# Seven half products for eight in five projections of the last two token groups

## The chip, the cores and the metric

The kernel runs on one core of a Trainium2 chip. The metric is device time in microseconds for one execution. A core has TensorE (matmuls, PE in the profile), VectorE (DVE), ScalarE (ACT), GpSimd (POOL) and SyncE (SP), which issues all DMAs of this kernel. Each engine works through its own instructions in order; they meet through semaphores.

## What is computed

One step of a decoder layer on 2,064 prompt positions (16 meta tokens among them) and 8 x 8 sampled ones, model width 1,024, all in fp32. Cut to what matters here:

```python
proj = rmsnorm(h, norm_gain) @ w_in             # 1024 -> 6 x 1024
u_s, z_s, u_p, z_p, gates = split(proj)         # gates = sigmoid(.. + b_gate) -> g_s, g_p
y_s = ssm_branch(u_s)                           # scan, gelu, y * sigmoid(y @ w_glu + b_glu)
y_p = pool_branch(u_p)                          # running means over 2, 4, 8, 16 rows, a 256 x 256 mix each
merged = g_s * ((y_s * silu(z_s)) @ w_branch_ssm) + g_p * ((y_p * silu(z_p)) @ w_branch_pool)
out = rmsnorm(h + merged @ w_out, final_norm_gain)
```

The projections for u_p, z_p, z_s, g_p and g_s are those that the change touches.

## The kernel before

**Tiling.** Features lie on the 128 partitions, tokens on the free axis. The tokens are four groups (g0 to g3, `GROUPS`) of 544, 536, 536 and 512 columns. An output block of 128 features of a projection is one *unit*: eight input blocks, three matmuls each (`mm3`), since every fp32 operand is split in a high and a low part and high x high, high x low and low x high are summed. A group of 536 columns is done as two outputs of 268, so a unit is 48 matmuls; the group of 512 takes 24. Results go to a PSUM tile `acc` of [128, 2, 512] f32, of which there are three (`acc`, `proj`).

**Weights.** The weights of each unit come from HBM as one raw tile of 512 KB (`w_load`, three buffers), ScalarE writes the high part (`w_high`, L105, tile wh), VectorE the low part (`w_low`, L207, tile wl), three buffers each. For unit i+2, `w_high` stands at the start of unit i and `w_low` at its end, and the load of unit i+5 at its end.

**Order.** All instructions are written in one hand-made order. `units` lists the matmul units. For each the main loop writes: `w_high` of the unit two ahead, the post work of the unit before (PSUM to SBUF, nonlinearity), events (`at`), and the unit's matmuls, between which `between` places small steps at given fractions (`at_part`).

**Stages of a group.** `u_pool`: units up (u), zp (z), the first gates (g) and the mixes (m) in the order of `ORDER`; a whole pooling of an up block on VectorE is written in one go in the post work (`up_post`), and the pooled block is split two units later (`po_split`). `u_pgate`: branch products brp with the remaining gates. `u_zs`: zs, with the GELU of the state-space output beside it (ScalarE, VectorE and GpSimd in a chain). `u_rest`: glu, gates gs with products brs, and eight out units, in which the inputs of the next group are normalised and split (`x_norm`); the norm of the outputs follows two units later. The final division goes with the next group's first units.

**State-space rounds.** The scan over groups 0 and 1 is round 0, that over groups 2 and 3 round 1. A round is 38 ticks of small matmuls and steps on all engines, spread over units by `spread`. Round 1 runs from the end of g0 to the `u_pgate` stage of g2, with weight 0 (BB) in the pool stages: 98 units that count.

## Time and profile before

| | us |
|---|---|
| runs (3) | 2111.9, 2112.03, 2113.97 |
| median | 2112.03 |
| profiled execution | 2110.94 |
| its span, first to last instruction | 2109.2 |

In that span TensorE was busy for 2068.6 us (98%), VectorE for 1311.9 (62%), ScalarE for 1007.5 (48%), GpSimd for 541.0 (26%); the mean granted TensorE clock was 0.995. A busy share says how much of the time an engine had an instruction in it. Matmuls overlap, so the length of one is longer than its spacing to the next; the spacing is what counts in a row of them. Groups 2 and 3 fill about the last 850 us: up to some 1680 us matmuls of 268 columns, from there of 512.

### The profile page before, as it was taken

How to read it: one execution, taken by the hardware profiler on the slowest of the kernel's cores; microseconds unless marked ns; L12 is line 12 of the kernel's file. 1: busy time of each engine (PE TensorE's matmuls, PEld its weight loads, DVE VectorE, ACT ScalarE, POOL GpSimd, SP SyncE). 2: the span in 40 equal slices, each digit the busy share in tenths (PEclk: the TensorE clock that was granted, in tenths of full speed). 3: DMA queues.
4: the chain of work that ended last, by engine and by line, in shares of the span. 5: the costliest groups of instructions: out<-in, count | busy, mean ns of one | idle time of the engine just before them, and what ended most of it. 6: DMA issues, size and time to landing. Idle time of an engine off the chain costs nothing.

```text
span 2109.2 us, 37669 instructions
## 1 busy us (share of the span) xinstructions
PE 2068.6 (98%) x14968; PEld 1960.0 (93%) x14968; DVE 1311.9 (62%) x1844; ACT 1007.5 (48%) x1579; POOL 541.0 (26%) x718
## 2 busy tenths in 40 slices
PE   7999999999999999999899999999999999999998
PEld 7998899998999999999899999999999988888887
DVE  6879858898655776546755776535533667345344
ACT  5334469877555553356665553324332333234322
POOL 1156525463422330023422330012100210022001
PEclk9999999999999999999999999999999999999999
DMA  5435557587534643245444533334233443343333
GB/s 202 145 124 171 172 163 212 158 244 203 156 92 143 177 135 121 91 124 141 119 128 147 166 117 127 96 116 125 91 106 124 134 133 105 108 144 105 100 99 101
DMA packets 226095, 288.30 MB, mean 137 GB/s; under 512 B 111744, under 2 KB 156160, under 8 KB 225920
## 3 DMA queue, kind: packets, MB, share of 16 engines
q1 hardware_dynamic: 225920, 285.90, 44.8%
q8 instruction: 118, 1.93, 0.4%
q14 instruction: 57, 0.47, 0.1%
HBM read 242.58 MB, written 40.89 MB: 134 GB/s over the span
## 4 chain that ended last, share of the span: by engine, by line
PE 85%; DVE 5%; ACT 4%; DMA 2%; issue 2%; POOL 1%; SPq 0%; DVEq 0%; ACTq 0%; POOLq 0%
PE acc L128 27%; PE acc L132 27%; PE acc L130 27%; PE ps_k L408 1%; PE sx L519 1%; PE sy L589 1%; PE sy L590 1%; ACT wh L105 1%; DVE sX L549 1%; DVE w L951 1%; DVE wl L207 0%; DMA ys<-sS 0%; DVE sph L506 0%; DMA smc<-mat_d 0%; DVE sX L537 0%
## 5 line engine op out<-in xcount | busy, mean ns | idle before, releaser
L128 PE MATMUL acc<-ah,wh 128*128 128x268 f32 (+4 forms) x4504 | 1055.2, 304 | 9.1 <-ACT wh L105 7.8
L132 PE MATMUL acc<-ah,wl 128*128 128x268 f32 (+4 forms) x4504 | 1045.7, 302 | 0.0
L130 PE MATMUL acc<-al,wh 128*128 128x268 f32 (+4 forms) x4504 | 1044.4, 301 | 0.0
L128 PEld LDWEIGHTS acc<-ah,wh 128*128 128x128 f32 x4504 | 726.2, 189 | 43.2 <-issue 8.0
L105 ACT ACTIVATE wh<-raw 128x1024 fp32r<-128x1024 f32 (+1 forms) x336 | 347.3, 1034 | 854.5 <-PE acc L130 559.8
L132 PEld LDWEIGHTS acc<-ah,wl 128*128 128x128 f32 x4504 | 725.1, 189 | 27.1
L130 PEld LDWEIGHTS acc<-al,wh 128*128 128x128 f32 x4504 | 725.4, 189 | 26.7 <-DVE al L720 0.2
L207 DVE TENSOR_TENSOR wl<-raw,wh 128x1024 fp32r<-128x1024 f32 (+1 forms) x336 | 421.6, 1256 | 139.4 <-ACT wh L105 138.2
L541 POOL TENSOR_TENSOR sXw<-sXw,sph 128x270 f32<-128x270 f32 (+1 forms) x64 | 46.5, 726 | 362.5 <-ACT sXw L527 362.3
L872 DVE SCALAR_TENSOR_TENSOR H<-H,acc 128x536 f32<-128x536 f32 (+2 forms) x64 | 44.9, 702 | 85.8 <-ACT H L871 85.7
L970 DVE SCALAR_TENSOR_TENSOR H<-po,H 128x536 f32<-128x536 f32 (+2 forms) x32 | 22.7, 711 | 111.2 <-ACT po L968 107.5
L946 POOL TENSOR_SCALAR w<-w 128x536 f32<-128x536 f32 (+2 forms) x32 | 27.0, 845 | 227.6 <-ACT w L945 227.4
L114 DVE TENSOR_TENSOR al<-H,ah 128x536 fp32r<-128x536 f32 (+3 forms) x96 | 77.4, 842 | 7.7 <-ACT ah L105 6.7
L537 DVE TENSOR_TENSOR sX<-sx,scc 128x270 f32<-128x270 f32 (+1 forms) x64 | 27.1, 423 | 85.9 <-ACT sxs L530 59.9
L549 DVE TENSOR_TENSOR_SCAN sX<-r,state,sX 128x135 f32<-128x135 f32 (+1 forms) x128 | 72.8, 609 | 2.3
L1011 POOL TENSOR_TENSOR ss<-ss,po 128x536 f32<-128x536 f32 (+2 forms) x25 | 41.8, 1673 | 125.6 <-ACT po L1007 107.0
L827 POOL COPY hist<-E 128x16 f32<-128x16 f32 x24 | 15.6, 651 | 218.8 <-ACT E L817 218.8
L836 DVE TENSOR_TENSOR w<-E 128x483 f32<-128x483 f32 (+2 forms) x32 | 22.6, 708 | 78.8 <-ACT E L817 54.4
L981 DVE SCALAR_TENSOR_TENSOR sg<-sg,acc 128x536 f32<-128x536 f32 (+2 forms) x32 | 22.4, 701 | 78.1 <-PE acc L132 78.1
L105 ACT ACTIVATE ah<-H 128x536 fp32r<-128x536 f32 (+3 forms) x80 | 50.2, 644 | 43.1 <-DVE H L902 31.9
L923 DVE SCALAR_TENSOR_TENSOR G<-sg,acc 128x536 f32<-128x536 f32 (+2 forms) x32 | 22.4, 701 | 74.9 <-PE acc L132 70.9
L103 POOL TENSOR_SCALAR ah<-G 128x536 fp32r<-128x536 f32 (+2 forms) x16 | 14.9, 943 | 193.2 <-DVE sg L981 150.8
(231 smaller groups left out, 2216.3 us busy)
## 6 DMA issues: line engine op xcount, KB each, us to landing
raw<-in_wb SPq DMA_DIRECT2D x318, 512.0 KB, 3.8
smc<-mat_d SPq DMA_DIRECT2D x64, 256.0 KB, 3.6
smb<-mat_d SPq DMA_DIRECT2D x64, 128.0 KB, 2.5
xr<-in_xb SPq DMA_DIRECT2D x21, 268.0 KB, 4.2
H<-in_xb SPq DMA_DIRECT2D x19, 268.0 KB, 4.4
ys<-sS SPq DMA_DIRECT2D x32, 135.0 KB, 4.4
us<-po SPq DMA_DIRECT2D x16, 268.0 KB, 4.6
su<-us SPq DMA_DIRECT2D x64, 67.0 KB, 2.6
```

Source lines behind the costliest of these rows:

```text
L105: A.activation(out, in_, AF.Copy)
L114: V.tensor_tensor(l, x, h.bitcast(F32), ALU.subtract)
L128: PE.matmul(out, wh, xh, start=first, stop=False)
L130: PE.matmul(out, wh, xl, start=False, stop=False)
L132: PE.matmul(out, wl, xh, start=False, stop=last)
L207: V.tensor_tensor(l[:, c], r[:, c], h[:, c].bitcast(F32), ALU.subtract)
L537: V.tensor_tensor(d["x"], d["px"][:, :, :g.kp], d["c"][:, :, 1:g.kp + 1], ALU.mult)
L541: G.tensor_tensor(d["xw"], d["xw"], d["s"][:, :, 1:g.kp + 1], ALU.mult)
L549: V.tensor_tensor_scan(x[:, j], r8[:, i].to_broadcast([P, g.kp]), x[:, j], state[:, i], ALU.mult, ALU.add)
L872: V.scalar_tensor_tensor(self.v3(out), self.v3(out), 1.0, self.pv(ps), ALU.add, ALU.mult)
L946: G.tensor_scalar(q, q, 0.044715, 1.0, ALU.mult, ALU.add)
L1011: (G if h is None else V).tensor_tensor(self.ss[:, c], self.ss[:, c], s, ALU.add)
```

## The change

For groups 2 and 3 the units of the five projections go in pairs of output blocks. A pair is a product of 2 x 2 blocks: two output blocks, two halves of the eight input blocks, two halves of the tokens (268 or 256 columns). Seven products of half size take the place of eight, on sums and differences of the operands.

- **Weights** (`ws_load`, `ws_sum`): for each pair VectorE makes four sums of weight blocks, in 40 jobs between the end of g0 and g1's first glu units, and stores them to DRAM (`ws_d`). A pair is four units of kind s (t = 0 to 3), the first three with a full tile of weights, the last with half; `w_load` gathers each from one to three DMAs.
- **Inputs** (`s_op`, `x_scale`): in the brs and out units of the group before, VectorE and ScalarE prepare seven input operands (b11, t1, t2, b22, t3, b21, t4) in place of one split.
- **Products** (`s_unit`): accumulators a and b are the two halves of one acc tile, c half of a second. a takes b11, t2, t3 and t4 in turn, and ScalarE copies it out after each of the first three (p1, u2, u3); c takes t1 (copied to p5) and b22; b takes b21. VectorE and ScalarE combine these in the post work.
- **Order** (`u_fast_pool`): pool stage by `FAST_ORDER`, with the zs pairs 0 and 1 moved into it; pooling is issued in single steps, 1.3 us apart by the plan's own lengths (`up_step`); zs pairs 2 and 3 follow the brp units. `w_low` of s units stands at 0.6 of the unit.
- **State-space round 1** now ends in g1 (77 units that count), its buffers are freed for the new tiles, and `final_states` runs in g1's first out unit.

**TensorE, g2, units zp 0 and up 1, before**: 48 matmuls a unit, then the next unit into another acc tile (ah, al: input parts, wh, wl: weight parts; the waits are for an engine's semaphore).

```order
L128 MATMUL acc_15154<-ah_14593,wh_15011 128x268 [waits DVE_49,Activation_49]
L128 MATMUL acc_15154<-ah_14593,wh_15011 128x268
L130 MATMUL acc_15154<-al_14594,wh_15011 128x268 x2
L132 MATMUL acc_15154<-ah_14593,wl_15066 128x268 x2
...
L128 MATMUL acc_15218<-ah_14593,wh_15070 128x268 [waits PE_49,Activation_49]
L128 MATMUL acc_15218<-ah_14593,wh_15070 128x268
L130 MATMUL acc_15218<-al_14594,wh_15070 128x268 x2
L132 MATMUL acc_15218<-ah_14593,wl_15125 128x268 [waits DVE_49]
```

**The same place after, pair zp 0 (g2)**: tile acc_15779 holds a and b, acc_15780 is c; the products b11, t1, t2, b22, t3, b21, t4 begin in this order.

```order
L136 MATMUL acc_15779<-ah0_15274,wh_15715 128x268
...
L136 MATMUL acc_15780<-ah0_15274,wh_15715 128x268 [waits PE_49]
...
L136 MATMUL acc_15779<-t2h_15370,wh_15750 128x268 [waits Activation_49]
...
L136 MATMUL acc_15780<-ah_15183,wh_15750 128x268 [waits Activation_49]
...
L136 MATMUL acc_15779<-t43h_15367,wh_15771 128x268 [waits Activation_49]
...
L136 MATMUL acc_15779<-ah_15183,wh_15771 128x268 [waits Activation_49]
...
L136 MATMUL acc_15779<-t43h_15367,wh_15819 128x268 [waits DVE_49]
```

Each product of 12 matmuls begins with a row shown. The waits of the third and fifth are for copies of a, of the fourth for that of c. The sixth, into b, waits for ScalarE's copy of a (u3), the seventh, into a, for VectorE's subtract L805, which reads b.

**ScalarE, g2, post work of zp 1 and up 2, before** (wh: weight split, H: zp result or pooled split, E: up result).

```order
L105 ACTIVATE wh<-raw 128x1024 [waits DVE_49,DMAHW0_49,PE_49,Activation_49]
L871 ACTIVATE H_15340<-acc 128x536 [waits PE_49]
L105 ACTIVATE H_15345<-po 128x536 [waits DVE_49]
L105 ACTIVATE wh<-raw 128x1024 [waits DMAHW2_49,PE_49,Activation_49]
L817 ACTIVATE E<-acc 128x4x67 [waits PE_49,Pool_49]
L817 ACTIVATE E<-acc 128x4x67
L105 ACTIVATE wh<-raw 128x1024 [waits DVE_49,DMAHW4_49,PE_49,Activation_49]
```

**ScalarE after, from pair zp 0 (t=1) into pair up 1 (t=1)** (u, p: copies of accumulators, rs: Tanh results).

```order
L775 ACTIVATE u_15839<-acc 128x268 [waits PE_49]
L112 ACTIVATE wh<-raw 128x1024 [waits DMAHW4_49,DMAHW3_49,DMAHW5_49,PE_49,Activation_49]
L112 ACTIVATE H_15878<-po 128x536 [waits DVE_49]
L775 ACTIVATE u_15885<-acc 128x268 [waits PE_49]
L112 ACTIVATE wh<-raw 128x1024 [waits DMAHW0_49,DMAHW7_49,PE_49,Activation_49]
L112 ACTIVATE wh<-raw 128x1024 [waits DMAHW2_49,DMAHW1_49,DMAHW3_49,PE_49,Activation_49]
L811 ACTIVATE H_15782<-acc 128x268 [waits DVE_49,PE_49]
L828 ACT_TABLE_LOAD
L828 ACTIVATE rs<-H_15781 128x536
L828 ACTIVATE rs<-H_15782 128x536 [waits DVE_49,Activation_49]
L775 ACTIVATE p_15952<-acc 128x268 [waits PE_49]
L112 ACTIVATE wh<-raw 128x512 [waits DMAHW5_49,PE_49]
```

Copies for which TensorE waits (u, p) now stand behind splits of pooled values (H<-po) that wait for VectorE, and behind a table load and two Tanh.

The diff, cut to its core:

```diff
+FAST_ORDER = "U0 Z0 U1 m0 Z1 U2 m1 S0 Z2 U3 m2 S1 Z3 G0 m3"
+STEP = 1.3
...
-    def mm3(outs, w, xs, first, last):
+    def mm3(outs, w, xs, first, last, more=False):
...
-            PE.matmul(out, wh, xh, start=first, stop=False)
+            PE.matmul(out, wh, xh, start=first, stop=False, skip_group_check=more)
...
+    ws_d = {w: dram.tile([NB // 2, 2, P, 4, 256], F32, name=f"ws{w}") for w in W_FAST}
...
+        if kind == "s":
+            base, p, t = i
+            a1, a2 = a["wb"][base + 2 * p], a["wb"][base + 2 * p + 1]
+
+            def sums(out, *js):
+                o = out.rearrange("p (j h c) -> p j h c", j=len(js), h=2)
+                for h in range(2):
+                    SY.dma_start(o[:, :, h], ws_d[base][p, h][:, js[0]:js[-1] + 1])
+
+            if t == 0:
+                SY.dma_start(r[:, :512], a1[:, :512])
+                sums(r[:, 512:], 3)
+            elif t == 1:
+                sums(r, 0, 1)
+            elif t == 2:
+                sums(r[:, :512], 2)
+                SY.dma_start(r[:, 512:], a1[:, 512:])
+            else:
+                SY.dma_start(r[:, :512], a2[:, 512:])
...
+    def ws_load(base, p, h):
+        x, y = (tmp.tile([P, 2, 256], F32, tag="rs", bufs=2, name="ws") for _ in range(2))
+        for r, t in enumerate((x, y)):
+            SY.dma_start(t, a["wb"][base + 2 * p + r].rearrange("p (j h c) -> p j h c", j=2, h=2)[:, :, h])
+        sums[base, p, h] = (x, y)
+
+    def ws_sum(base, p, h):
+
+
+
+        x, y = sums.pop((base, p, h))
+        V.tensor_tensor(y[:, 1], y[:, 1], y[:, 0], ALU.add)
+        V.tensor_tensor(y[:, 0], y[:, 0], x[:, 0], ALU.add)
+        V.tensor_tensor(x[:, 0], x[:, 0], y[:, 1], ALU.add)
+        V.tensor_tensor(x[:, 1], x[:, 1], x[:, 0], ALU.add)
+        for j, t in ((0, x), (2, y)):
+            SY.dma_start(ws_d[base][p, h][:, j:j + 2], t)
...
+        def s_banks(self):
+            t, c = self.acc(), self.acc()
+            return [x[:, :self.H2] for x in (t[:, 0], t[:, 1], c[:, 0])]
+
+        def s_mm(self, out, w, j, x, first, pos):
+            xh, xl = self.op[x]
+            for k in range(4):
+                between(pos + k / 8)
+                mm3([out], [v[:, 512 * j + k * P:512 * j + (k + 1) * P] for v in w], [(xh[k], xl[k])],
+                    first and k == 0, k == 3, not first)
+
+        def s_keep(self, name, bank):
+            t = sw["r"].tile([P, self.H2], F32, tag=name, bufs=1, name=name)
+            A.activation(t, bank, AF.Copy)
+            self.d[name] = t
...
+        def s_unit(self, name, p, t, w):
+            if t == 0:
+                self.d = dict(zip("abc", self.s_banks()))
+                self.d["to"] = getattr(self, "to_" + name)(p)
+            d = self.d
+            a_, b_, c_, to = d["a"], d["b"], d["c"], d["to"]
+            if t == 0:
+                self.s_mm(a_, w, 0, "b11", True, 0)
+                self.s_keep("p1", a_)
+                self.s_mm(c_, w, 1, "t1", True, 0.5)
+                return lambda: self.s_keep("p5", c_)
+            if t == 1:
+                self.s_mm(a_, w, 0, "t2", False, 0)
+                self.s_keep("u2", a_)
+                self.s_mm(c_, w, 1, "b22", False, 0.5)
+
+                def post():
+                    for o, v in to(0, 1):
+                        V.tensor_tensor(o, v(c_), v(d["u2"]), ALU.subtract)
+                return post
+            if t == 2:
+                self.s_mm(a_, w, 0, "t3", False, 0)
+                self.s_keep("u3", a_)
+                self.s_mm(b_, w, 1, "b21", True, 0.5)
+
+                def post():
+                    for o, v in to(0, 0):
+                        V.tensor_tensor(o, v(b_), v(d["p1"]), ALU.subtract)
+                return post
+            self.s_mm(a_, w, 0, "t4", False, 0)
+
+            def post():
+                for o, v in to(1, 0):
+                    A.activation(o, v(a_), AF.Copy)
+                for o, v in to(1, 1):
+                    V.tensor_tensor(o, v(d["u3"]), v(d["p5"]), ALU.subtract)
+                for j in range(2):
+                    getattr(self, "fin_" + name)(2 * p + j)
+            return post
...
+        def fin_silu(self, s, q):
+            A.activation(q, s, AF.Tanh, scale=0.5)
+            V.scalar_tensor_tensor(s, q, 1.0, s, ALU.add, ALU.mult)
+
+        def fin_zp(self, f):
+            self.fin_silu(self.sz[f], self.t(tmp, "rs", 2))
...
+        def fin_gate(self, f, b):
+            A.activation(self.sg[f], self.sg[f], AF.Tanh, scale=0.5, bias=hb[:, b, f:f + 1])
...
+        def x_scale(self, k):
+            x = self.xr[k]
+            V.scalar_tensor_tensor(x, x, sm[:, GAIN, k:k + 1], self.rs, ALU.mult, ALU.mult)
...
+        def s_op(self, k, part):
+
...
+            n = self.H2
+            x, y = self.xr[k], self.xr[k + 4]
+            x1, x2, y1, y2 = x[:, :n], x[:, n:], y[:, :n], y[:, n:]
+            op = self.op
+            if part == 0:
+                h, l = self.slot(self.sa, k + 4, y, "a")
+                op["b21"][0][k], op["b21"][1][k] = h[:, :n], l[:, :n]
+                op["b22"][0][k], op["b22"][1][k] = h[:, n:], l[:, n:]
+                flush()
+                V.tensor_tensor(y2, x2, y2, ALU.subtract)
+                V.tensor_tensor(x2, x2, x1, ALU.subtract)
+            elif part == 1:
+                h, l = (self.tx(self.sa, f"{c}{k}", 1, F32R) for c in ("ah", "al"))
+                A.activation(h, x, AF.Copy, scale=-1.0)
+                V.scalar_tensor_tensor(l, x, -1.0, h.bitcast(F32), ALU.mult, ALU.subtract)
+                op["b11"][0][k], op["b11"][1][k] = h[:, :n], l[:, :n]
+                op["t1"][0][k], op["t1"][1][k] = h[:, n:], l[:, n:]
+                V.tensor_tensor(x1, x1, y2, ALU.subtract)
+                V.tensor_tensor(y1, y1, x1, ALU.subtract)
+            else:
+                r = sw["r"]
+                h, l = (r.tile([P, self.C], F32R, tag=f"{c}{k}", bufs=1, name=c) for c in ("t43h", "t43l"))
+                split(h, l, y, "a")
...
+                h, l = (r.tile([P, n], F32R, tag=f"{c}{k}", bufs=1, name=c) for c in ("t2h", "t2l"))
+                split(h, l, x1, "a")
+                op["t2"][0][k], op["t2"][1][k] = h, l
+                self.xr.pop(k), self.xr.pop(k + 4)
...
+        def up_step(self, fb):
+            if fb not in self.q:
+                self.q[fb] = self.up_pool(fb, self.E[fb])
+            if next(self.q[fb], 0) == 0:
+                self.q.pop(fb)
+                self.E.pop(fb)
...
-                ps = self.acc()
+                ps = sw["m"] if self.fast and j == 0 else self.acc()
...
+    def u_fast(g, base, name, p):
+
+        for t in range(4):
+            i = add("s", (base, p, t), g.s_unit, name, p, t)
+        return i - 3, i
...
+    def u_fast_pool(g):
+
+        pools, gelus = [], None
+        for unit in FAST_ORDER.split():
+            kind, p = unit[0], int(unit[1])
+            if kind == "U":
+                lo, i = u_fast(g, W_UP, "up", p)
+                if g.last:
+                    for j in range(2):
+                        at(lo - 2, g.hs_load, 2 * p + j)
+                pools.append((i + 1, p))
+            elif kind == "Z":
+                u_fast(g, W_ZP, "zp", p)
+            elif kind == "S":
+                u_fast(g, W_ZS, "zs", p)
+            elif kind == "G":
+                u_fast(g, W_GP, "gp", p)
+            else:
+                add("m", p, g.mix, p)
+        n = len(units)
+        for f in range(NB):
+            add("w", W_BRP + f, g.brp, f)
+            if f % 2 == 0 and f < 6:
+                u_fast(g, W_GP, "gp", f // 2 + 1)
+        m = len(units)
+        zs = [u_fast(g, W_ZS, "zs", p)[1] for p in (2, 3)]
+        for i, p in pools:
+            t = 0.6
+            for f in (2 * p, 2 * p + 1):
+                for _ in range(p + 2):
+                    after(g, i, t, g.up_step, f)
+                    t += STEP
+                after(g, i, t, g.po_split, f)
+                after(g, i, t, flush)
+                t += STEP
+        for f in range(NB):
+            t = 9.0 * f
+            after(g, n, t, g.y_load, f, f"H{f}", 1)
+            after(g, n, t + 6, g.y_gelu1, f)
+            after(g, n, t + 11, g.y_gelu2, f)
+            after(g, n, t + 16, g.y_gelu3, f)
+            after(g, m, 0.5 + 1.6 * f, g.y_split, f)
+            after(g, m, 0.5 + 1.6 * f, flush)
+        i = len(units) - 1
+        for f in range(NB):
+            at((zs[0] - 1 if f < 4 else zs[0] + 3 if f < 6 else zs[1] + 2) + f % 2, g.y_gate, f)
+
...
-        for f in range(ahead, 3 if ahead else 2):
-            add("w", W_GS + f, g.gate, f, 0)
+        if g.fast:
+            u_fast(g, W_GS, "gs", 0)
+        else:
+            for f in range(ahead, 3 if ahead else 2):
+                add("w", W_GS + f, g.gate, f, 0)
...
                 at(b, nxt.x_load, f)
+                if nxt.fast:
+                    if f == 0:
+                        at(b, nxt.rs_load)
+                    at(b + 2, nxt.x_scale, f)
...
-            if f + ahead < NB:
+            if g.fast:
+                if f % 2 == 0 and f < 6:
+                    _, last_gs = u_fast(g, W_GS, "gs", f // 2 + 1)
...
-            if nxt:
+            if nxt and nxt.fast:
+                if f == 0 and nxt is g2:
+                    at(i, final_states)
+                    at(i + 1, end_ssm)
+                for part in range(3):
+                    if 0 <= f - 2 - part < 4:
+                        at_part(i, 0.3 * part, nxt.s_op, f - 2 - part, part)
...
         if nxt:
             at(i + 2, g.norm)
             for k in range(NB):
-                at(i + 3 + k, g.final, k)
+                at(i + 3 + (2 if nxt.fast else 1) * k, g.final, k)
...
+    def end_ssm():
+        sw["endps"].close()
+        sw["end"].close()
+        _par.close()
+        sw["r"] = ctx.enter_context(tc.tile_pool(name="r", bufs=1))
+        pm = ctx.enter_context(tc.tile_pool(name="pm", bufs=1, space=PSUM))
+        sw["m"] = pm.tile([P, 2, 512], F32, name="pm")
...
-    for g, nxt in ((g1, g2), (g2, g3), (g3, None)):
-        n = len(units)
-        u_pool(g)
-        busy |= set(range(n, len(units)))
-        hi = u_pgate(g)
-        if g is g2:
-            spread(rounds[1], i + 2, hi, busy, BB)
-        u_zs(g, range(NB), True)
+    n, first = len(units), i
+    u_pool(g1)
+    busy = set(range(n, len(units)))
+    u_pgate(g1)
+    u_zs(g1, range(NB), True)
+    end = len(units) + NB + 2
+    u_rest(g1, g2, 0)
+    spread(rounds[1], first + 2, len(units) - NB - 1, busy, BB)
+
+
+    todo = [(w, p, h) for w in W_FAST for p in range(NB // 2) for h in range(2)]
+    free = [j for j in range(first + 3, end) if not n - NB - 2 < j < n + 1]
+    for k, job in enumerate(todo):
+        j = free[k * len(free) // len(todo)]
+        at(j, ws_load, *job)
+        at_part(j, 0.9, ws_sum, *job)
+    for g, nxt in ((g2, g3), (g3, None)):
+        u_fast_pool(g)
         u_rest(g, nxt, 0)
-    at(hi, final_states)
...
-        mid.append((1, w_low, (ahead,)))
+        mid.append((0.6 if key[0] == "s" else 1, w_low, (ahead,)))
```

## Rows read from the trace of the kernel before

**Rows 1.** Busy time by stretch: us, PE, PEld, DVE, ACT, POOL, clock, DMA, GB/s
```profile
1250.00:1680.00 430.00, 430.00 (x3490) 430.00 (x3490) 220.83 (x277) 147.08 (x206) 49.77 (x57) 1.00 0.37 114
1680.00:2080.00 400.00, 400.00 (x1751) 325.25 (x1750) 202.48 (x260) 136.09 (x188) 52.35 (x65) 1.00 0.36 113
```

**Rows 2.** Timeline of TensorE: start, length (us), operation; groups 2 and 3, and the end
```profile
1500.16 0.41 PE L128 MATMUL acc<-ah,wh 128*128 128x268 f32 x2
...
1507.58 0.41 PE L128 MATMUL acc<-ah,wh 128*128 128x268 f32 x2
...
2071.84 0.39 PE L130 MATMUL acc<-al,wh 128*128 128x512 f32 x1
...
2077.86 0.39 PE L128 MATMUL acc<-ah,wh 128*128 128x512 f32 x1
...
2080.64 0.28 PE L128 MATMUL acc<-ah,wh 128*128 128x256 f32 x1
...
2090.41 0.28 PE L132 MATMUL acc<-ah,wl 128*128 128x256 f32 x1
```

**Rows 3.** Timeline: who starts when its releaser ends (in brackets: idle before, releaser)
```profile
304.75 0.44 DVE L537 TENSOR_TENSOR sX<-sx,scc 128x270 f32<-128x270 f32 x1 [1.79 <-ACT sXw L527]
...
305.24 0.73 PE L519 MATMUL sx<-su,smb 128*128 128x135 f32 x4 [0.92 <-DVE sX L537]
...
2083.34 0.28 PE L132 MATMUL acc<-ah,wl 128*128 128x256 f32 x1
2083.66 0.42 DVE L1000 SCALAR_TENSOR_TENSOR G<-acc,xr 128x256 f32<-128x256 f32 x1 [0.73 <-PE acc L132]
...
2099.09 0.42 ACT L1007 ACTIVATE po<-G 128x256 f32<-128x256 f32 x1 [1.07 <-DVE G L1000]
2099.56 0.70 PE L1041 MATMUL acc<-po,onesm 128*128 128x256 f32 x2 [0.53 <-ACT po L1007]
```

**Rows 4.** Groups by shape: busy us, mean ns of one, idle before
```profile
L105 ACT ACTIVATE wh<-raw 128x1024 fp32r<-128x1024 f32 x318 | 336.1, 1057 | 802.0 <-PE acc L130 549.1 <-issue 251.5 <-ACT H L105 0.7
...
L817 ACT ACTIVATE E<-acc 128x268 f32<-128x268 f32 x32 | 10.6, 381 | 0.0
L952 ACT ACTIVATE w<-w 128x536 f32<-128x536 f32 x16 | 10.5, 653 | 14.6 <-DVE w L951 14.6
...
L137 ACT ACT_TABLE_LOAD x7 | 9.0, 1283 | 0.1
...
L207 DVE TENSOR_TENSOR wl<-raw,wh 128x1024 fp32r<-128x1024 f32 x318 | 406.6, 1280 | 139.4 <-ACT wh L105 138.2
...
L207 DVE TENSOR_TENSOR wl<-raw,wh 128x512 fp32r<-128x512 f32 x18 | 15.0, 837 | 0.0
L537 DVE TENSOR_TENSOR sX<-sx,scc 128x270 f32<-128x270 f32 x32 | 13.9, 433 | 25.9 <-ACT sXw L527 25.7
```

**Rows 5.** Busy time by stretch, in and after the first state-space round, and group 1
```profile
150.00:200.00 50.00, 50.00 (x401) 42.49 (x399) 47.34 (x54) 23.73 (x37) 31.23 (x29) 1.00 0.57 169
400.00:450.00 50.00, 47.37 (x378) 46.20 (x377) 43.60 (x70) 42.43 (x83) 28.02 (x44) 1.00 0.74 213
1050.00:1250.00 200.00, 200.00 (x1629) 199.85 (x1629) 123.57 (x172) 114.69 (x187) 59.66 (x91) 1.00 0.48 144
```

**Rows 6.** DMA issues, from the page: KB each, median us from issue to landing
```profile
raw<-in_wb SPq DMA_DIRECT2D x318, 512.0 KB, 3.8
```

**Rows 7.** TensorE waits on the timeline, their sum (us, times, longest), clock behind them
```profile
300.68 0.73 PE L519 MATMUL sx<-su,smb 128*128 128x135 f32 x4 [1.45 <-DVE sX L537]
...
1027.52 0.56 PE L589 MATMUL sy<-su,smc 128*128 128x131 f32 x2 [2.17 <-ACT sS L595]
...
PE sy L589 <- ACT sS L595: 6.1, 3, 3.8
...
300.00:304.00 4.00, 3.32 (x27) 3.32 (x28) 2.74 (x5) 2.88 (x6) 1.97 (x3) 1.00 0.23 59
1027.80:1031.20 3.40, 3.40 (x18) 3.40 (x18) 2.68 (x7) 3.26 (x8) 2.80 (x6) 0.50 0.49 124
```

129 lines of the change are left out of this document (101 added, 28 removed).

## Prediction

> **What bounds the kernel now.** I read first the busy time of each engine in long stretches, then single matmuls on the timeline, then how one engine releases another, last the waits and the clock. In the stretches that hold token groups 2 and 3, TensorE is busy for all of 430 and all of 400 us at a granted clock of 1.00, with VectorE at about 51% and ScalarE at 34% [rows 1]. No TensorE wait is listed from 1030 us to the end of that second stretch. So there the time is the number of matmuls times their spacing, and whatever makes TensorE wait is added in full.
>
> The spacing comes from starts on the timeline [rows 2]. From 1500.16 to 1507.58 lie 60 matmuls of 268 columns: 7.42 / 60 = 0.1236 us. From 2071.84 to 2077.86 lie 26 of 512 columns: 0.2315 us. From 2080.64 to 2090.41 lie 83 of 256 columns, each with other weights and into one accumulator as in the new code: 0.1177 us. A row's own length is longer (0.28 for 256 columns; 0.41 - 0.124 = 0.29 for 268), since each overlaps the next.
>
> **The matmuls removed.** Five projections of four output pairs are 20 pairs a group. Group 2 (268 columns): a pair falls from 96 to 84 matmuls, 20 x 12 x 0.1236 = 29.7 us. Group 3: a pair falls from 48 of 512 columns (11.11 us) to 84 of 256 (9.89 us), 20 x 1.22 = 24.5 us. Together **-54.2 us**.
>
> **Two waits that every pair gains.** The seven products share three accumulators a, b, c, and a and b are the two halves of one acc tile. The order of the changed program, quoted above, has two waits per pair that the data do not ask for. The first matmul into b (unit t=2) waits for ScalarE's copy u3, which reads a. The first matmul of t=3 into a waits for VectorE's subtract (L805), which reads b. Both readers can start only when the matmuls just ahead have ended, so neither can be done early; all 40 pairs have both.
>
> Price of one, from last matmul start to next start. TensorE's matmul of 256 columns starting at 2083.34 ends at 2083.62, and VectorE starts at 2083.66: 0.04. ScalarE ends at 2099.51, TensorE starts at 2099.56; VectorE ends at 305.19, TensorE starts at 305.24: 0.05 each [rows 3]. A ScalarE copy of 268 columns takes 0.38, a VectorE operation with a 270-column accumulator 0.43 [rows 4]; I take 0.42 for 268, and 0.37 and 0.41 for 256. First wait, group 2: 0.29 + 0.04 + 0.38 + 0.05 - 0.124 = 0.64; second 0.68. Group 3: 0.62 and 0.66. Sum 20 x 1.32 + 20 x 1.28 = **+52.0 us**. This is the price with both engines idle when TensorE ends, so it is nearly the least it can be; what is queued ahead comes on top. The two halves lie 512 f32 apart in a partition. The Trainium skill (PSUM — Partial Sum Buffer, Terms) says that a bank holds 512 f32 per partition and that it is within one bank that two engines must not meet; by that, the halves are two banks, the chip asks for neither wait, and the sum would be about -52 us. No row of before has a tile used in this way, and the waits stand in the program all the same: I go by them.
>
> **What else the pairs ask of the queues.** Each pair splits 3.5 weight tiles in place of 2. In group 2's pool stage (11 pairs and 4 mixes, 11 x 10.38 + 4 x 2.97 = 126 us of matmuls) VectorE does 33 splits of 1024 and 15 of 512, 33 x 1.28 + 15 x 0.84 = 55 us, and 33 half-width combinations, 14 us [rows 4], beside the pooling, mixing, gating and normalising work as before. I put it at 110 to 125 us, against 126 plus 14 of waits: it fits, but a subtract for which TensorE waits now stands behind a split of 1.2 us or a pooling step, and ScalarE's copies stand behind splits of pooled values that wait for VectorE. The bounds are two stretches of before: at 150 us VectorE was busy for 47.3 of 50 and TensorE lost nothing; at 400 us VectorE at 43.6 and ScalarE at 42.4 of 50, chained to each other, cost TensorE 2.6 of 50, 5% [rows 5]. The pool stage is chained like the second: 5% of 140 is 7 us a group, **+14** (0 to 28).
>
> Smaller ones. At three places a group a pair follows a mix, whose post work (two VectorE scalings, two ScalarE splits of 0.65) ends at about 2.7 us of a 2.97 us unit before the copy p1 is needed: nothing if VectorE is on time, 0.7 if it is 1 us behind; +3. The pairs behind two Tanh (seven a group): 1.06 + 0.38 + 2 x 0.65 + 0.38, less 0.08 of overlap at each step, ends at about 2.9: +1.5 (0 to 4). Accumulator c of a pair reuses the tile that a was copied from: ready at 1.5 us, wanted at 1.48; +2 (0 to 4). The norm of the group before now falls two short units, not two long ones, behind its last matmul, and its two table loads of 1.28 [rows 4] on ScalarE stand ahead of copies u2 and p1 that TensorE waits for: about 2.4 a group, +5 (0 to 8).
>
> Weight transfers: nine issues a pair instead of two, and 1.79 MB per 10.4 us where 1.05 MB per 11.8 us was. A tile is asked for two units ahead, at least 1.48 + 2.97 = 4.45 us, and lands in 3.8 [rows 6]; ScalarE needs it a unit before TensorE does. I cost it at nothing; cover gone, each late tile is 1 us or so.
>
> **Group 1.** The 40 weight sums are four VectorE adds of 256 each, about 0.43 [rows 4], 1.7 us a job in some 64 units. VectorE's load in this stretch is 124 of 200 us [rows 5], so it rises to about 80%; where a sum waits for its load, all behind it waits, but a weight split there has a whole unit (5.9 us) of slack. The second state-space round is packed from 98 to 77 units, four ticks instead of three in the eight zs units, and there ticks already make TensorE wait: 6.1 us in three waits, after two of which (2.17 us is one) the clock stood at 0.50 for some 3.4 us [rows 7]. One more such place, and more delay: +6 (-9 to +20). Operand preparation, the final states and the pooling in steps lie under TensorE's work in the out and pool stages, whose cost is in the 14.
>
> **Sum.** -54.2 + 52.0 + 14 + 3 + 1.5 + 2 + 5 + 6 = **+29 us**. The profiled execution took 2110.94 us (span 2109.2), 1.1 below the median of 2112.03. From the median: 2141, and I say **2140 us**.
>
> **Rivals.**
> (a) *The waits eat the gain and nothing comes on top.* VectorE and ScalarE are idle when TensorE ends in nearly every pair, as at 150 us: 2112 - 2 + 0 to 6, **2112 us**. For it: VectorE has time on average. Against it: queues in order, and both engines' loads rise.
> (b) *Faster: the ticks come apart from the GELU chain.* The second round's ticks are redistributed in group 1's zs units. If none meets the ScalarE-VectorE chain of the GELU there, the 6.1 us of waits and two half-clock stretches (each 3.4 us at 0.50 costs 1.7) go, 9.4 us: 2112 - 2.2 - 9.4 = **2100 us**. It decides once everything queued on top in groups 2 and 3 stays under 5 us. Against it: more ticks, not fewer, in those units, and VectorE busier.
> (c) *The clock falls.* Two waits of 0.7 us lie within 3 us of every pair, longer with a queue ahead. Single waits of up to 1.45 us left the clock at 1.00, one of 2.17 us was followed by 0.50 for 3.4 us [rows 7]. If half of the 40 pairs lose 1.7 us in this way it is +34 on the forecast, if all, +68: **2175 to 2210 us**. The Trainium skill (TensorE: Matmul & The Clock Gate, A second HAM failure mode: psum-queue depth-cycling) tells of a kernel that idled briefly and often between groups of matmuls and swung between full and half clock; no run here yet shows repeated short waits.
>
> **How the numbers follow.** Forecast (2118 to 2175): 0.66. (a): 0.13. (b), or waits priced too high: 0.11. (c): 0.10. The range 2106 to 2185 leaves out most of (b) and the upper part of (c); its ends are the sum with all queueing at nothing and group 1 a little better, and with queueing at its upper bounds. A measurement of this kernel tells about 0.2% (4 us) from no change: faster 0.11, same 0.13, slower 0.76.
>
> **What would show it.** In the profile of the changed kernel: TensorE matmul counts lower by 240 in group 2, spacing 0.124 and 0.118; TensorE waits for ScalarE's L775 and VectorE's L805, at least 40 of each, idle about 0.5 us apiece (the rest of the 0.65 is the tail counted as busy); granted clock near 1.00 in groups 2 and 3. If those waits are missing or short, the second term falls and the time is nearer 2060 to 2090. If the clock stands well under 1.00, it is (c). If TensorE waits for wl or wh instead, VectorE or the transfers bound the stage.

## The result and the profile after

The changed kernel takes **2261.6 us** (median of 4, 2255.8 to 2264.4) against 2112.2 for the kernel before (median of 4): a ratio of 1.070, interval 1.068 to 1.072. The forecast was 2140 with a range to 2185: the right side, and a fifth of the size. The profiled execution took 2261.3 us, span 2259.5.

Where the 150.3 us between the two spans lie is read from three places: the start of group 2 (before: the last output update of group 1 on VectorE, released by the last matmul of that unit, TensorE's next unit beginning 0.2 us ahead of it, at 1242.5; after: the first TensorE row of single matmuls of 268 columns), the start of group 3 (the first matmul of another width), and the end. Timelines, start, length, operation; first the kernel before, then the changed one:

```profile
1242.70 0.72 DVE L997 SCALAR_TENSOR_TENSOR G<-acc,xr 128x536 f32<-128x536 f32 x1 [3.85 <-PE acc L132]
...
1685.27 0.39 PE L128 MATMUL acc<-ah,wh 128*128 128x512 f32 x1
```

```profile
1323.41 0.29 PE L136 MATMUL acc<-ah,wh 128*128 128x268 f32 x1
...
1790.45 0.28 PE L136 MATMUL acc<-ah,wh 128*128 128x256 f32 x1
```

| stretch | before | after | difference | forecast |
|---|---|---|---|---|
| up to the start of group 2 | 1242.5 | 1323.4 | +80.9 | +6 |
| group 2 | 442.8 | 467.0 | +24.2 | about +9 |
| group 3 and the end | 423.9 | 469.1 | +45.2 | about +14 |

(The forecasts of the two groups are its saving, its two waits and half of its 25.5 us of queueing each.) So more than half of the loss stands where the change leaves every projection as it was. The boundary moves a little work too: 32 tick matmuls of the second state-space round stand in group 2 before and in group 1 after, 3.6 us (before_pack below has a group 2 of 439.2). For equal work the first two differences are some 77 and 28.

TensorE's waits in the changed kernel, from 560 us (the second state-space round has begun) to group 2, then from there on (us in total, times, longest):

```profile
PE sx L571 <- DVE sX L589: 20.0, 11, 6.2
PE sy L641 <- ACT sS L647: 19.3, 5, 9.3
PE acc L140 <- DVE wl L239: 11.7, 10, 4.8
PE acc L136 <- ACT ah L112: 6.2, 2, 5.0
```

```profile
PE acc L136 <- ACT u L775: 27.1, 42, 2.5
PE acc L136 <- ACT p L775: 14.1, 12, 2.0
PE acc L136 <- DVE E L805: 13.3, 10, 4.1
PE acc L136 <- DVE sg L805: 10.6, 16, 1.2
PE acc L975 <- POOL ss L1252: 8.8, 2, 4.9
```

In the stretch of the first list the kernel before waits 8.8 us in five places; here the first four lines alone make 57.2. The second list has what the prediction looked for (L775, L805), and a third thing, GpSimd.

**Group 1.** The waits of VectorE and of the DMA queue SP in group 1 name the cause (ws: the raw weights of a weight sum; L254 the first add of a job, L257 the last, L259 the store; L589 and L620 are state-space steps):

```profile
DVE ws L254 <- DMA ws<-in_wb: 139.0, 38, 7.2
...
SPq L259 <- DMA ws<-in_wb: 115.2, 40, 5.0
SPq L259 <- DVE ws L257: 89.9, 31, 4.5
```

The page gives these loads 4.6 us from issue to landing. One job on the timelines of SP (load, store), VectorE (adds), ScalarE and TensorE:

```profile
1040.19 1.32 SPq L246 DMA_DIRECT2D ws<-in_wb  x2
1047.48 0.80 SPq L259 DMA_DIRECT2D ws<-ws  x2
```

```profile
1040.10 0.72 DVE L121 TENSOR_TENSOR al<-xr,ah 128x536 fp32r<-128x536 f32 x1
1045.66 0.42 DVE L254 TENSOR_TENSOR ws<-ws 128x256 f32<-128x256 f32 x1 [4.84 <-DMA ws<-in_wb]
...
1047.37 1.22 DVE L239 TENSOR_TENSOR wl<-raw,wh 128x1024 fp32r<-128x1024 f32 x1
...
1049.13 0.71 DVE L1192 SCALAR_TENSOR_TENSOR xr<-w,xr 128x536 f32<-128x536 f32 x1
```

```profile
1042.48 1.04 ACT L112 ACTIVATE wh<-raw 128x1024 fp32r<-128x1024 f32 x1
...
1049.88 0.65 ACT L112 ACTIVATE ah<-xr 128x536 fp32r<-128x536 f32 x1 [5.85 <-DVE xr L1192]
...
1052.73 0.37 ACT L647 ACTIVATE sS<-sy 128x262 f32<-128x262 f32 x1
```

```profile
1053.16 0.81 PE L641 MATMUL sy<-su,smc 128*128 128x131 f32 x2 [9.26 <-ACT sS L647]
```

The load is issued at 1040.19; VectorE is through with its earlier work at 1040.8 and stands 4.84 us for it. The weight split that the program has behind the adds starts at 1047.37, 3.9 us after ScalarE had its high part ready (1043.52), and the GELU step L1192 behind that at 1049.13. ScalarE waits 5.85 us for this step; its step of the state-space tick (L647) stands behind its GELU work, and TensorE waits 9.26 us for it at 1053. So this job puts the chain off by some 4 us; what makes up the rest of the 9.26 is not taken apart here. SP meanwhile has the job's store at the head of its queue and issues nothing from 1041.5 to 1047.5. The Trainium skill (PSUM — Partial Sum Buffer, Engine vs sequencer instructions) says that the queues of ScalarE, VectorE and GpSimd are strictly first in, first out; the trace agrees: the weight split, its input ready at 1043.52, does not pass the adds that wait until 1045.66.

**A pair without any queueing.** This is gp pair 1 of group 2, the last two products, on TensorE, ScalarE and VectorE:

```profile
1499.38 0.28 PE L140 MATMUL acc<-t43h,wl 128*128 128x268 f32 x1
1500.14 0.39 PE L136 MATMUL acc<-ah,wh 128*128 128x268 f32 x1 [0.48 <-ACT u L775]
1500.38 0.28 PE L138 MATMUL acc<-al,wh 128*128 128x268 f32 x1
...
1501.60 0.28 PE L140 MATMUL acc<-ah,wl 128*128 128x268 f32 x1
1502.49 0.39 PE L136 MATMUL acc<-t43h,wh 128*128 128x268 f32 x1 [0.60 <-DVE sg L805]
1502.72 0.29 PE L138 MATMUL acc<-t43l,wh 128*128 128x268 f32 x1
```

```profile
1499.70 0.39 ACT L775 ACTIVATE u<-acc 128x268 f32<-128x268 f32 x1 [0.50 <-PE acc L140]
```

```profile
1502.00 0.44 DVE L805 TENSOR_TENSOR sg<-acc,p 128x268 f32<-128x268 f32 x1 [1.54 <-PE acc L140]
```

Both engines are idle when TensorE ends, as the prediction assumed; ScalarE starts 0.04 us behind that end, VectorE 0.12. The starts are 0.76 and 0.89 us apart, not 0.124, and the matmul after each comes 0.24 and 0.23 later: 0.64 + 0.11 and 0.77 + 0.11, 1.62 us a pair. In group 3 it is some 1.6.

### The profile page after: what moved, and what is told of

It reads as the page before. It is cut to its first block, busy times and chain, and to the rows that moved or that the text cites. A ratio compares the mean times of both kernels' runs of the same rounds, so it can differ in the third digit from the quotient of the medians.

```text
span 2259.5 us, 40543 instructions
## 1 busy us (share of the span) xinstructions
PE 2080.5 (92%) x15448; PEld 1983.8 (88%) x15448; DVE 1504.9 (67%) x2264; ACT 1141.4 (51%) x1852; POOL 527.8 (23%) x718
## 5 line engine op out<-in xcount | busy, mean ns | idle before, releaser
L136 PE MATMUL acc<-ah,wh 128*128 128x268 f32 (+4 forms) x4184 | 993.6, 300 | 54.5 <-ACT u L775 24.2
L140 PE MATMUL acc<-ah,wl 128*128 128x268 f32 (+4 forms) x4184 | 977.3, 296 | 11.7 <-DVE wl L239 11.6
L138 PE MATMUL acc<-al,wh 128*128 128x268 f32 (+4 forms) x4184 | 978.0, 296 | 0.9 <-DVE al L121 0.7
L112 ACT ACTIVATE wh<-raw 128x1024 fp32r<-128x1024 f32 (+1 forms) x416 | 414.7, 997 | 710.8 <-PE acc L138 537.2
L138 PEld LDWEIGHTS acc<-al,wh 128*128 128x128 f32 x4184 | 694.5, 191 | 14.7 <-DVE al L121 1.2
L239 DVE TENSOR_TENSOR wl<-raw,wh 128x1024 fp32r<-128x1024 f32 (+1 forms) x416 | 504.2, 1215 | 66.6 <-ACT wh L112 65.8
L136 PE MATMUL acc<-t43h,wh 128*128 128x268 f32 (+1 forms) x320 | 96.8, 302 | 36.4 <-DVE E L805 13.3
L254 DVE TENSOR_TENSOR ws<-ws 128x256 f32<-128x256 f32 x40 | 17.9, 448 | 139.0 <-DMA ws<-in_wb 139.0
L136 PEld LDWEIGHTS acc<-t43h,wh 128*128 128x128 f32 x320 | 61.2, 191 | 45.4 <-DVE E L805 15.4
L140 PE MATMUL acc<-t43h,wl 128*128 128x268 f32 (+1 forms) x320 | 92.2, 288 | 0.3 <-DVE wl L239 0.2
L138 PE MATMUL acc<-t43l,wh 128*128 128x268 f32 (+1 forms) x320 | 92.2, 288 | 0.0
L641 PE MATMUL sy<-su,smc 128*128 128x135 f32 (+1 forms) x256 | 52.4, 286 | 22.1 <-ACT sS L647 20.7
```

Source lines behind the costliest of these rows:

```text
L112: A.activation(out, in_, AF.Copy)
L136: PE.matmul(out, wh, xh, start=first, stop=False, skip_group_check=more)
L138: PE.matmul(out, wh, xl, start=False, stop=False, skip_group_check=more)
L140: PE.matmul(out, wl, xh, start=False, stop=last, skip_group_check=more)
L239: V.tensor_tensor(l[:, c], r[:, c], h[:, c].bitcast(F32), ALU.subtract)
L641: PE.matmul(d["py"][:, j], d["m"][:, 0, m], d["u"][:, j], start=True, stop=False)
```

## The experiments

Each kernel is the changed one with the edit shown, unless it says otherwise. Medians of the runs; the kernel before took 2111.7 to 2114.3 beside them. The stages, from the profiled execution of each:

| run | median | group 2 starts | group 2 | group 3 to end |
|---|---|---|---|---|
| before | 2112 | 1242.5 | 442.8 | 423.9 |
| changed | 2261.6 | 1323.4 | 467.0 | 469.1 |
| swap | 2214.5 | 1316.5 | 444.4 | 449.3 |
| late | 2210.8 | 1274.5 | 467.2 | 465.9 |
| ws | 2189.1 | 1252.7 | 469.1 | 465.8 |
| norm | 2256.2 | 1321.3 | 468.6 | 467.1 |
| keep | 2266.6 | 1323.1 | 475.3 | 467.3 |
| best | 2142.1 | 1255.3 | 445.1 | 442.0 |
| three | 2148.2 | 1248.8 | 440.7 | 449.3 |
| quad | 2124.4 | 1255.6 | 435.6 | 435.2 |
| relief | 2120.9 | 1251.3 | 431.2 | 435.0 |
| g2only | 2117.9 | 1253.9 | 432.4 | 427.8 |
| g2only_wl35 | 2122.1 | 1257.3 | 435.2 | 427.8 |
| before_ws | 2174.7 | 1305.4 | 442.8 | 423.9 |
| before_pack | 2113.3 | 1250.8 | 439.2 | 423.9 |

The expectations below speak of 77 us for group 1 and of 439 for group 2 of the kernel before: they took its group 2 to start at 1246.5, 4 us later than here.

**Which half of the change costs group 1 its time: before_ws and before_pack.** The kernel before, once with the weight sums alone (the new functions and their placing, as in the diff), once with the packed second round alone (before_pack's edit is shown):

```diff
-        if g is g2:
-            spread(rounds[1], i + 2, hi, busy, BB)
         u_zs(g, range(NB), True)
         u_rest(g, nxt, 0)
+        if g is g1:
+            spread(rounds[1], i + 2, len(units) - NB - 1, busy, BB)
+            hi = len(units) - NB
```

> The kernel before with the 40 weight-sum jobs (loads, four VectorE adds each, stores) at the same places in group 1, and nothing else; the sums are not used. The changed kernel reaches group 2 some 77 us later than the kernel before. Theory 2 (VectorE and the DMA queue SP each stand at a job until its load, issued at the head of the same unit, has landed, and the state-space ticks and weight splits queue behind): most of the 77 us, so 45 to 75 us over before, 2157 to 2187. Rival (it is the second state-space round, packed from 98 into 77 units): under 10 us, 2112 to 2122.

> The kernel before with its second state-space round spread over the units from the end of group 0 to group 1's last glu and brs units, as in the changed kernel, final states at group 1's first out unit, and nothing else. Theory 2 (weight sums): 0 to 15 us over before, 2112 to 2127. Rival (packing): 45 to 75 us, 2157 to 2187. If both theories hold half, 25 to 40 each.

before_ws: 2174.7 us, +62 (ratio 1.029, 1.028 to 1.031). before_pack: 2113.3, ratio 1.0004 (0.9994 to 1.0013), no difference in the whole. The weight sums are the cause: alone they put off the start of group 2 by 62.9 of the 80.9 us. The packed round alone puts it off by 8.3, of which 3.6 leave group 2 in exchange, in a profiled execution that is 2.4 us above its median. The 10 us that are left show only with both together. VectorE's and SP's waits in before_ws are those of the changed kernel over again:

```profile
DVE ws L225 <- DMA ws<-in_wb: 149.0, 38, 7.9
...
SPq L230 <- DMA ws<-in_wb: 112.2, 38, 5.0
```

The 40 jobs' own adds are 40 x 1.7 = 68 us of VectorE; the next two runs tell the adds from the waiting.

**late and ws: the same loads, adds and stores, placed apart.**

```diff
-        at_part(j, 0.9, ws_sum, *job)
+        at(j + 1, ws_sum, *job)
```

> The changed kernel with each weight sum (and its store) moved from 0.9 of the unit that issues its load to the head of the next unit, behind the post work there: same loads, adds and stores, but VectorE would wait for TensorE's end of the unit there anyway, so the load's 4.6 us lie under that. Theory 2: VectorE's 139 us of waits for these loads mostly go, and the time falls by 25 to 60 us, to some 2202 to 2237; not all, since a store still stands in SP's queue ahead of other loads. Rival (packing): falls by less than 10 us, 2252 or more.

late: 2210.8, -51 us, as theory 2 has it. For ws the store also got a function of its own, and the jobs other places (two units apart, none in the zs units that hold ticks):

```diff
-        at(j, ws_load, *job)
-        at_part(j, 0.9, ws_sum, *job)
...
+        at(j, ws_load, *job, own)
+        at(j + 1, ws_sum, *job)
+        at_part(j + 1, 0.6, ws_store, *job)
```

> The changed kernel with the three steps of a weight-sum job pulled apart: load at the head of a unit, adds at the head of the next, stores at 0.6 of that, so that neither VectorE nor the DMA queue stands at a step whose forerunner has just been issued; jobs on the same buffers two units apart, eight jobs on two idle input tiles, none in the zs units with the ticks. Theory (all of group 1's 77 us are these two in-order waits): group 2 starts 60 to 75 us earlier than in the changed kernel, 2262 falls to 2187 to 2202, below the 2211 of the run that moved only the adds and stores together. Rival (the adds themselves, 40 x 1.8 us on a VectorE that has little left, cost the rest): no better than 2205 to 2215.

ws: 2189.1, -72.5 us; group 2 starts at 1252.7, 10 us behind the kernel before and 2 behind before_pack, with every add still there. What was left of VectorE's waits for these loads, in late and in ws:

```profile
DVE ws L254 <- DMA ws<-in_wb: 44.1, 17, 5.7
```

```profile
DVE ws L255 <- DMA ws<-in_wb: 29.2, 17, 5.5
```

So of 80.9 us about 10 stay with the adds, their traffic, the operands and the packed round all in place; about 70 hung on where load, adds and store stand. The adds' place gave 49 of them (group 2 starts at 1274.5 in late). The other 22 came with the stores apart and the jobs out of the tick units, which no run tells from each other.

**swap: the two waits of each pair.**

```diff
-            return [x[:, :self.H2] for x in (t[:, 0], t[:, 1], c[:, 0])]
+            return [x[:, :self.H2] for x in (t[:, 0], c[:, 1], c[:, 0])]
```

> The changed kernel with one line different: accumulator b is the second half of c's acc tile, no longer of a's. Then b21 waits only for VectorE's read of c, half a unit back, and t4 only for ScalarE's copy u3, which has the 12 matmuls of b21 to end in. Theory 1 (the two waits of each pair are in the program because a and b share a tile, and they are on TensorE's path): the changed kernel's trace has 0.64 + 0.11 and 0.76 + 0.11 us of extra spacing at these two places in an undisturbed pair, 1.62 us, times 40 pairs = 65 us; the time falls from 2262 by 50 to 68, to about 2197. Rival: the waits stand in front of work that ScalarE and VectorE must do anyway before the next products, so the next wait grows by half of it; the time falls by 20 to 40, to about 2230. If the chip itself keeps the two halves of a tile apart in some other way the time moves by less than 10.

2214.5, -47 us: between the two expectations. Groups 2 and 3, where the edit acts, are 42.4 us shorter; the other 5 or so lie ahead of them, where the two programs are the same. In an undisturbed pair both waits are gone; the same gp pair's first matmul and the first of the unit behind it:

```profile
1475.12 0.28 PE L136 MATMUL acc<-ah,wh 128*128 128x268 f32 x1
...
1485.48 0.41 PE L136 MATMUL acc<-ah,wh 128*128 128x268 f32 x2
```

84 matmuls in 10.36 us, 0.1233 each. So 40 x 1.6 = 64 us of waits went, and some 22 came back. TensorE's waits from group 2 on show where, the copies p1 and p5 (14.1 us in 12 before this edit):

```profile
PE acc L136 <- ACT p L775: 30.0, 23, 4.2
PE acc L136 <- ACT u L775: 3.2, 2, 1.8
```

**norm, keep, best, three.** The norm of the group before, later:

```diff
-            at(i + 2, g.norm)
+            at(i + (5 if nxt.fast else 2), g.norm)
...
```

> The changed kernel with the norm of the group before issued five short units behind its last out unit instead of two, the final divisions three later too, and nothing else. In the changed kernel's trace TensorE stands 4.9 and 4.1 us in the first pair of groups 2 and 3, for GpSimd's sum of squares. Theory (that is a wait of its own): the two stalls go, -8 to -11, 2251 to 2254. Rival (the sum of squares is late for a reason that holds later work too, or the wait returns at the next copy): under 4 us.

2256.2, -5.5 us by the medians, between the two; its runs (2253.7 to 2258.9) overlap those of the changed kernel, and groups 2 and 3 together are 0.4 us shorter in the profiled execution, so a gain in these stages is not shown. The two waits for GpSimd's sum (8.8 us) are gone; in group 2 one of 3.3 us has come in the same pair, at the third product, and the waits for the copies u and p, 41.2 us in the changed kernel, are 49.2. That is the rival's mechanism: the wait returns at the next copies.

keep turns ScalarE's order in the pair units round:

```diff
-        w_high(ahead)
+        short = units[i][0][0] == "s" and units[i][0][1][2] < 3
+        if not short:
+            w_high(ahead)
...
+            mid.append((0.51, w_high, (ahead,)))
```

> The changed kernel with ScalarE's order within a unit of the pairs turned round: the copy of an accumulator first, then the weight split of the unit two ahead, the split of a pooled value, the mix's post work and the Tanh of the pair before; weight low parts at 0.9 of the unit. Theory (in the pool stages TensorE waits for copies queued behind work that itself waits for VectorE or a transfer: the idle at the third, fourth and fifth product sums to about 20 us in the changed kernel's trace): falls by 10 to 20 us, to 2242 to 2252. Rival (ScalarE and VectorE lack the time as such, or the later weight splits make TensorE wait for wl): within 6 us of 2262 or slower.

2266.6, +5 with overlapping runs: the rival, no gain. TensorE's waits from group 2 on, to be held against the list of the changed kernel: copies of u fall from 27.1 to 19.6 us, none over 0.7, but the waits for the subtractions on VectorE (L806 here) rise from 33.5 to 48.6 us over their five outputs; two of them:

```profile
PE acc L136 <- ACT u L776: 19.6, 40, 0.7
PE acc L136 <- DVE sg L806: 13.4, 16, 1.1
PE acc L136 <- DVE H L806: 11.7, 8, 2.4
```

All four edits together, and the three without keep:

> All four edits in one: b in c's tile, weight sums pulled apart, norm later, copies first. If they are separate terms: -47 (measured) - 60 to 75 - 8 to 11 - 20 to 35 (the copies' idle is 38 us in the run with b moved) from 2262 gives 2094 to 2127, at the best below the 2112 of the kernel before. If the edits pay for the same idle twice: 2130 to 2150.

> The changed kernel with three of the four edits (b in c's tile, weight sums pulled apart, norm later), ScalarE's order as in the changed kernel. If the edits are separate terms: 2262 - 47 - 72.5 - 5.5 = 2137, and since the run of all four gave 2142, the turned ScalarE order costs some 5 here as it did alone. Rival (turned order helps once b is moved): 2150 or more.

best: 2142.1, in the second of its ranges, since the 20 to 35 us of keep did not come. three: 2148.2, its runs spread from 2140.6 to 2150.4; the median is 113 us under the changed kernel where the three edits add up to 125 (2137), and so nearer to the rival's 2150. Whether keep helps or harms beside them these two do not tell, since their runs overlap.

**quad: more time between a product and the next into its accumulator.** Three edits (the norm one unit less late), and two pairs interleaved unit by unit in the pool stage and for zs pairs 2 and 3:

```diff
-FAST_ORDER = "U0 Z0 U1 m0 Z1 U2 m1 S0 Z2 U3 m2 S1 Z3 G0 m3"
+FAST_ORDER = "Z0 Z1U0 S0U1 m0 Z2U2 m1 S1U3 m2 Z3G0 m3"
...
         for t in range(4):
-            i = add("s", (base, p, t), g.s_unit, name, p, t)
+            for q, (base, name, p) in enumerate(ps):
+                add("s", (base, p, t), g.s_unit, name, p, t, q)
```

> As the run with three edits, but in the pool stages and for the last two zs pairs two pairs are interleaved, unit by unit (P t=0, Q t=0, P t=1, ...; the second pair's c and b in the PSUM tile that only the mixes used), so that between a product into an accumulator and the next into it lie some 4.4 us, not 1.5; the pool stage begins with zp 0 alone. Theory (what is left in the pool stages, 35 us in group 2 and 41 in group 3 of the run with all four edits, is latency: copies and subtractions queued for 1 to 3 us behind other work of ScalarE and VectorE while TensorE has only 1.5 us of other work): most of it goes, 2137 falls by 30 to 55, to 2082 to 2107, below the kernel before. Rival (VectorE lacks the time in these stages: it is busy to three quarters and every wait just moves): falls by less than 15, or other waits appear (weight low parts), 2122 or more.

2124.4: 24 us below three by the medians, 12.5 by the profiled executions. By the time it is the rival, by the waits it is both. TensorE's waits from 1250 us on, in three and then in quad (1.5 us of the 14.7 lie ahead of group 2):

```profile
PE acc L136 <- ACT p L779: 32.6, 26, 3.8
PE acc L136 <- ACT u L779: 6.2, 4, 1.8
...
PE acc L140 <- DVE wl L239: 2.3, 3, 1.1
```

```profile
PE acc L140 <- DVE wl L239: 14.7, 18, 2.5
PE acc L136 <- DVE H L1147: 9.5, 6, 1.8
...
PE pm L136 <- ACT p L779: 2.6, 2, 2.3
PE acc L136 <- ACT p L779: 2.3, 1, 2.3
```

The copies are no longer waited for (38.8 us are 4.9); VectorE is, for weight low parts and the scaling behind a mix (L1147). Its load in quad's two pool stages (us, then busy PE, PEld, DVE, ACT, POOL, clock):

```profile
1300.00:1400.00 100.00, 92.12 (x723) 89.68 (x722) 81.31 (x133) 54.45 (x95) 6.90 (x13) 1.00 0.51 163
1700.00:1840.00 140.00, 124.86 (x928) 120.04 (x927) 107.13 (x187) 73.36 (x130) 15.88 (x32) 0.95 0.52 166
```

**relief, g2only, g2only_wl35.** Work taken from VectorE, then half products in group 2 alone, then low parts earlier:

```diff
-                    V.tensor_tensor(o, v(d["u3"]), v(d["p5"]), ALU.subtract)
+                    G.tensor_tensor(o, v(d["u3"]), v(d["p5"]), ALU.subtract)
...
+            if self.gi in (1, 2):
+                A.activation(o, o, AF.Copy, scale=sm[:, FGAIN, fb:fb + 1])
+                G.tensor_tensor(o, o, self.ss[:, c], ALU.mult)
```

> As the run with interleaved pairs, with work taken from VectorE in the pool stages: the difference of two copies (u3 - p5), the low parts of the t=3 weights and the final division's product go to GpSimd (the division's gain to ScalarE), the last out unit's post work goes behind the first copy, and the splits ahead of the first gs pair are spread over four units. Theory (VectorE's queue, busy 36 to 41 of 50 us in the pool stages of the interleaved run, is what is left there): some 16 of its 80 us a stage go to an engine busy for 2 to 6 of 50, the waits shrink by half, and the time falls from 2124 by 10 to 25, to 2099 to 2114, level with the kernel before or below it. Rival (GpSimd takes two to three times as long for the same step, and TensorE waits for it instead): 2120 or more.

```diff
-FAST = (2, 3)
+FAST = (2,)
```

> The run with VectorE relieved, but half products in group 2 alone; group 3's projections are eight products of 512 columns again, as in the kernel before. In the relieved run's trace group 2 takes 431 us where the kernel before takes 439, and group 3 takes 435 us where the kernel before takes 424. Theory (group 3's matmuls of 256 columns leave VectorE and ScalarE less time a pair, 9.9 us in place of 10.4, for the same copies, splits and pooling, so its 24.5 us are more than eaten): the time falls by 8 to 14 us, 2121 to 2107 to 2113, at the level of the kernel before (2112.5) or just under. Rival (group 3's loss hangs on the operands made ready in group 2's last units and the shorter first pairs, and returns as a slower end of group 2): 2116 or more.

```diff
-        mid.append((0.6 if key[0] == "s" else 1, w_low, (ahead,)))
+        mid.append((0.35 if key[0] == "s" else 1, w_low, (ahead,)))
```

> As the run with half products in group 2 alone, with the low parts of the pairs' weights issued at 0.35 of a unit in place of 0.6. TensorE waits for them 8 us in nine places in group 2's pool stage of the relieved run. Theory (they stand behind pooling steps that could wait): another 3 to 8 us, 2100 to 2108, 0.2 to 0.6% under the kernel before. Rival (VectorE's queue is full there, whatever comes first): within 3 us of the other run.

relief: 2120.9 (ratio 1.0042), -3.5, within the spread of quad's runs (2117.3 to 2130.1): the rival's time, though not by its mechanism, since in its profile TensorE waits for VectorE's low parts still:

```profile
PE acc L140 <- DVE wl L239: 18.0, 20, 2.5
```

VectorE is less busy than in quad: in the stretch from 1300 to 1400 us 72 of 100, where it was 81.

```profile
1300.00:1350.00 50.00, 45.18 (x344) 44.14 (x344) 35.18 (x50) 27.51 (x47) 16.97 (x19) 0.97 0.50 161
1350.00:1400.00 50.00, 46.21 (x361) 44.72 (x361) 37.27 (x61) 27.03 (x48) 11.81 (x12) 1.00 0.44 141
```

The waits for low parts did not fall with its load, so a lack of VectorE time is not shown to be their cause.

g2only: 2117.9, ratio 1.0028 (1.0017 to 1.0039), the nearest to the kernel before; group 3 gets 7 of its 11 us back, and the forecast of 2107 to 2113 is missed. g2only_wl35: 2122.1, 4 us slower, its group 2 2.8 us longer: low parts issued earlier at this place do not help. What holds them up stays open. No version here beats the kernel before. In g2only group 2 is 10.4 us shorter than before, 6.8 for equal work, of 29.7 us of matmuls removed; up to group 2 it is 11.4 longer.

## Why the prediction failed

**The saving** held: an undisturbed pair takes 10.36 us once its waits are gone (forecast 10.38), and g2only's group 2, 432.4 us, is 7 us under the 439.2 of before_pack, which holds the same work, with all that is left of the queueing.

**The two waits of each pair** were right in kind, place and count, and 1.62 us where 1.32 was priced. Two sizes were off: VectorE started 0.12 after TensorE's end (1501.88, then 1502.00), not the 0.04 of [rows 3], and TensorE needs 0.11 more for the matmul behind a wait, which no term had. Of the Trainium skill's rule quoted there (PSUM — Partial Sum Buffer, Terms): swap shows that the waits hang on the tile that a and b share, since they go when b stands in another; whether the chip would take the two halves of one tile at the same time no run here tests. The sum given with that rule, about -52, is wrong in itself: without the 52.0 the other terms add up to -23.

**Group 1** is the step that failed: "+6 (-9 to +20)", measured +81. It counted the adds (1.7 us a job) and gave the waiting no price: "where a sum waits for its load, all behind it waits, but a weight split there has a whole unit (5.9 us) of slack". The slack belongs to the weight split. The GELU steps and, through ScalarE, the state-space ticks behind the adds are waited for by TensorE within the unit (the 9.26 us above); and the store in SP's queue, which was not looked at, holds the next loads. All of it could be read ahead of the run: the load at the head of a unit, the add at 0.9 of the same unit, [rows 6] with 3.8 us for a load of this kind, and an engine that runs ahead of TensorE to the add. 40 jobs x 3.5 us of waiting is the 139 us of the trace. TensorE's own idle time rose by 55 us (63.8 against 8.8); most of the rest is the clock behind the long waits, 0.96 over this stretch where it was 0.99 before, some 24 us (an estimate from these two means and the lengths of the stretches, 764 and 682 us); in ws it is 1.00 again. The other half of that term, the packed round, was feared more and by itself costs nothing (before_pack).

**The queueing in the pool stages** (+14, with the smaller terms +25.5) came to about 63, the second step that was mis-sized. The pair stages are 24.2 + 45.2 = 69.4 us longer, 73.0 with the 3.6 of ticks that left group 2; the saving should have made them 54.2 shorter, and 64 is the price of the two waits: 73.0 + 54.2 - 64 = 63.2. Of it 9 is idle time at GpSimd's sum of squares; the prediction had priced that norm by its table loads and ScalarE alone. Some 14 is the clock (an estimate: 0.99 over 467 us and 0.98 over 456, where [rows 1] have 1.00). The bound of 5%, taken from the state-space round [rows 5], was too low for a chain in which TensorE has 1.5 us of other work and the copy behind it 1 to 3 us of queue. quad shows that the waits for copies are latency; what is then left is waits for VectorE's results, busy 81 of 100 us, and relief does not show that its load is the reason.

**The rivals.** (c) in part: the clock did fall, but behind single long waits and not, as forecast, by the 0.7 us waits of every pair (last section). (a) and (b) were out of the question once group 1 had lost 81 us; and (b)'s condition fails by itself, since with the packed round alone TensorE waits 9.6 us in seven places ahead of group 2, where it was 8.8 in five. The range's upper end, 2185, allowed group 1 no more than +20 (the upper bounds of all terms add up to 2177). With the wait priced at its whole as the upper bound, 40 x 3.8 = 152 us, the range's end is over 2300 and holds the time.

## What to carry to other kernels

An instruction that waits for a transfer, placed in a busy engine's queue shortly behind the issue of that transfer, is priced by the transfer and by everything behind it in that queue, not by its own duration; the store that follows does the same to the DMA queue. Here it paid to set load, use and store a unit or more apart, and the loads, adds and stores put alone into the old kernel told most of their price (62 of some 77 us). Half products also halve the time in which the steps between products can hide: ask what TensorE has left to do while a copy stands in another engine's queue, and what is the busiest engine after the saving.
